# Attention of the first query block and of the sample dealt into the input projection; the sample's tokens in the first block; values by features

## The chip, the cores and the metric

One core of a Trainium2 chip runs the whole program in one launch. Its engines are TensorE (PE; its weight loads are listed as PEld), VectorE (DVE), ScalarE (ACT), GpSimd (POOL) and SyncE (SP), which issues the DMAs. The metric is the device time of one execution in microseconds, the median of several runs.

## The reference

One layer of a hybrid encoder on 2048 prompt tokens and 32 sample tokens (model width 1024), all in f32:

```
h = x + RMSNorm(Mixer(RMSNorm(x)))
y = h + RMSNorm(ConvFFN(RMSNorm(h)))
Mixer:  proj = RMSNorm(x) @ w_in            -> q, k, v (512 each), z (512), xbc (768), dt (8)
  A: stick-breaking attention, 8 heads of 64: w = sigmoid(z_ij) * prod_{j<l<i} sigmoid(-z_il)
     prompt queries see earlier prompt keys, sample queries 2048 cached keys and earlier sample keys
  B: SSD: xbc -> causal conv (4 taps), SiLU -> x, B, C;  dt = softplus(dt + bias);
     h_t = exp(dt a) h + dt x B^T;  y = C h + D x;  y * silu(z), RMSNorm
  out = concat(RMSNorm(A), B) @ w_out
ConvFFN: (gelu(conv3(x @ w_gate)) * (x @ w_up)) @ w_down, hidden width 2816
```

Returned are y, the keys and values, the SSM state and the convolution histories, for prompt and sample.

## The kernel before

The 2080 tokens are handled in four blocks (`SBS`): three of 512 and a last one of 544, whose final 32 are the sample's. Activations lie by features: 128 features on the partitions, tokens along the free dimension. Every f32 operand is split into a high part and a rest (`xhi`, `xlo`, `whi`, `wlo`), and a product unit (`dense`, L118) takes 128 output features as 8 × 3 matmuls: for each of the 8 slices of the input width high × high, high × rest and rest × high. A 544-token block needs them twice, over 272 tokens each. `weight` (L98) loads such a unit's 512 KB into `wraw`, ACT rounds it to the high part (L108), POOL subtracts (L109).

The **input stage** (`phase_in`) does for each block: the split into parts (L272 f.); six units of `wbx` with the convolution and SiLU behind each (L324–346); the values and dt by tokens, the tokens of 128 being the stationary operand and 260 columns of `wv` moving (L365); the steps from dt to the cumulated decay, stored to DRAM (`acD`) and loaded back as a broadcast (`acB`, L426); SSD over four blocks of 128 tokens (L421–514): the decay matrix is `acB` minus `acum` (DVE L436), its exponential (ACT L440), times the masked C·B (L455, L458), then the products with x (L486) and the new state (`hT`, L498, L510), which the next block needs; the next block's squares, norm and normalisation in place (`prep`, L263); four units of `wk` and four of `wq`, each stored to DRAM; four units of `wz` with the gate (L557) and the gated norm. The last block's gate is not done there. It becomes a filler.

**Attention** then takes the blocks of queries one after the other (`heads`, L782). A slot is one head, 512 keys and 128 queries: two score matmuls into `z` (L811), two sigmoids on ACT (L659, L660), a reversed product scan on DVE (L662), a product on POOL or DVE (L667). Two slots later (`LOOK`) follow the transposes into `pt` (L832), a copy and, once per head, the value matmuls into `pa` (L847). Between slots `fill` hands out dense matmuls of the filler: the last gate under block 0, and under block s + 1 the output projection and feed-forward net of block s (`Tail.stream`). `sample` (L670) takes one step at every third slot of block 0. The last block's tail runs alone.

The order on each engine is made by a scheduler from this program order and the pools, except where `pin` ties filler matmuls to attention's. PSUM has eight banks of 512 columns: `o` has two for dense products; `in_psm` (`st`) two and `in_psy` (`y`) two of double size in the input stage; `z`, `pt` two each, `pa` and `u` one each in attention.

## Time and profile before

| | us |
|---|---|
| median of 3 runs (lowest, highest) | 3002.01 (3001.19, 3012.61) |
| profiled execution | 2999.56 |
| its span | 2997.4 |
| PE, DVE, ACT, POOL busy | 2839.3, 1567.7, 1239.6, 1254.8 |
| granted TensorE clock, mean | 0.979 |
| input stage of the four blocks | about 0 to 628 |
| heads of block 0, sample, last gate, first output products | about 628 to 800 |
| move to the tail of block 0 under block 1's heads | about 800 to 905 |
| heads of blocks 1 to 3 over the tails of blocks 0 to 2 | about 905 to 2478 |
| tail of block 3 alone | about 2478 to 2997 |

A row of a group reads: line, engine, operation, written tile <- read tiles, shapes, count | busy us, mean ns of one | idle us of the engine just before them and what ended it. A timeline row has start, duration, engine, line. A row of the chain has start, the time spent on the path, engine, tile, line. Matmuls are pipelined, so a mean of one in a group is longer than the distance at which they follow each other.

### The profile page before, as it was taken

To read this page: it belongs to the slowest core of one execution; us is meant where nothing else is said; L and a number is where in the kernel's file an instruction comes from. 1 tells how busy PE (TensorE), PEld (TensorE's weight loads), DVE (VectorE), ACT (ScalarE), POOL (GpSimd) and SP (SyncE) were. 2 spreads that over 40 slices of the span, in tenths; PEclk is the share of its full clock that TensorE was granted. 3 is DMA by queue.
4 is the path that set the end of the run, shared out by engine and by line. 5 is a ranking of instruction groups with operands and counts; after the bars stand their busy time and mean duration, and the time that the engine had idled before them with its cause. 6 is when DMAs were issued, how large, how long until landed. Compare 5 with 4: busy or idle time off the path is not lost.

```text
span 2997.4 us, 43276 instructions
## 1 busy us (share of the span) xinstructions
PE 2839.3 (95%) x16175; PEld 2320.3 (77%) x16175; DVE 1567.7 (52%) x2386; ACT 1239.6 (41%) x2514; POOL 1254.8 (42%) x1077
## 2 busy tenths in 40 slices
PE   8999899989979999999999999999999999899996
PEld 6777778866757778886677777856777779799996
DVE  7676676546574544337734344485444543523334
ACT  5344444346675544337533333564333433312111
POOL 4555555245666665536522222454122224511113
PEclk9999999989989999999999999999999999899998
DMA  5645453657657777876455545645544455554555
GB/s 172 183 145 177 144 169 106 185 150 248 241 178 242 246 250 266 289 265 203 158 190 176 184 156 208 232 163 174 177 165 167 157 196 191 192 188 167 178 178 171
DMA packets 234659, 571.58 MB, mean 191 GB/s; under 512 B 49514, under 2 KB 101362, under 8 KB 205906
## 3 DMA queue, kind: packets, MB, share of 16 engines
q1 hardware_dynamic: 234450, 568.81, 57.2%
q8 instruction: 129, 2.11, 0.3%
q14 instruction: 80, 0.66, 0.1%
HBM read 435.22 MB, written 133.50 MB: 190 GB/s over the span
## 4 chain that ended last, share of the span: by engine, by line
PE 72%; DVE 14%; DMA 6%; issue 3%; ACT 3%; POOL 2%; SPq 1%; DVEq 0%; POOLq 0%; ACTq 0%
PE o L124 36%; PE u L124 11%; PE t L124 10%; PE pa L847 4%; PE z L811 3%; PE pt L832 3%; DVE prow L662 2%; PE o L365 2%; DVE xc L341 2%; DVE acB L436 1%; DMA xr<-hS 1%; DMA acB<-acD 1%; DVE xc L337 1%; DVE x L263 1%; DMA w<-wS_out 1%
## 5 line engine op out<-in xcount | busy, mean ns | idle before, releaser
L124 PE MATMUL o<-xhi,w 128*128 128x512 f32 (+2 forms) x3968 | 1039.6, 346 | 28.4 <-ACT xhi L287 7.9
L124 PEld LDWEIGHTS o<-xhi,w 128*128 128x128 f32 x3968 | 696.5, 191 | 129.6 <-issue 10.1
L124 PE MATMUL o<-xlo,w 128*128 128x512 f32 (+2 forms) x1984 | 684.9, 345 | 9.4 <-DVE xlo L959 4.1
L109 POOL TENSOR_TENSOR w<-wraw,w 128x1024 fp32r<-128x1024 f32 (+2 forms) x156 | 370.6, 2376 | 256.1 <-ACT w L108 233.3
L124 PEld LDWEIGHTS o<-xlo,w 128*128 128x128 f32 x1984 | 379.6, 191 | 56.8 <-DVE xlo L959 7.6
L667 POOL TENSOR_TENSOR beta<-beta,prow 128x512 f32<-128x512 f32 (+3 forms) x256 | 255.7, 1000 | 377.4 <-DVE prow L662 345.2
L124 PE MATMUL u<-xhi,w 128*128 128x512 f32 x1056 | 345.8, 398 | 0.8 <-ACT r L201 0.5
L124 PE MATMUL o<-ah,w 128*128 128x512 f32 x992 | 335.9, 401 | 3.3 <-ACT f L1057 2.6
L1013 POOL TENSOR_TENSOR y<-y,gb 128x512 f32<-128x512 f32 (+1 forms) x88 | 115.5, 1313 | 511.2 <-ACT gb L1012 509.2
L662 DVE TENSOR_TENSOR_SCAN prow<-gam,prow,z 128x513 f32<-128x513 f32 x192 | 244.8, 1277 | 108.7 <-ACT beta L660 103.2
L124 PEld LDWEIGHTS u<-xhi,w 128*128 128x128 f32 x1056 | 198.5, 188 | 56.1 <-issue 5.6
L659 ACT ACTIVATE gam<-z 128x512 f32<-128x512 f32 (+2 forms) x320 | 173.3, 542 | 128.1 <-PE z L811 83.0
L124 PEld LDWEIGHTS o<-ah,w 128*128 128x128 f32 x992 | 187.1, 189 | 49.8 <-ACT f L1057 3.6
L124 PE MATMUL u<-xlo,w 128*128 128x512 f32 x528 | 209.3, 396 | 0.0
L835 ACT COPY wt<-pt 128x512 f32<-128x512 f32 (+3 forms) x282 | 148.1, 532 | 144.0 <-PE pt L832 141.3
L1005 DVE SCALAR_TENSOR_TENSOR y<-gb,cv,y 128x512 f32<-128x512 f32 (+1 forms) x176 | 162.3, 923 | 78.4 <-ACT y L1003 75.6
L108 ACT CAST w<-wraw 128x1024 fp32r<-128x1024 f32 (+2 forms) x156 | 155.2, 995 | 114.5 <-PE o L124 63.7
L124 PE MATMUL o<-al,w 128*128 128x512 f32 x496 | 196.5, 396 | 0.0
L124 PE MATMUL t<-xhi,w 128*128 128x272 f32 x960 | 189.1, 292 | 2.3 <-DMA w<-wS_up 2.0
L832 PEld LDWEIGHTS pt<-ident,beta 128*128 128x128 f32 x1088 | 132.4, 144 | 67.8 <-issue 27.5
L832 PE MATMUL pt<-ident,beta 128*128 128x128 f32 x1088 | 177.4, 282 | 6.4 <-POOL beta L667 3.9
L124 PE MATMUL t<-ah,w 128*128 128x272 f32 (+1 forms) x768 | 160.1, 302 | 17.4 <-ACT f L1057 7.5
(262 smaller groups left out, 4845.9 us busy)
## 6 DMA issues: line engine op xcount, KB each, us to landing
w<-wS_up SPq DMA_DIRECT2D x132, 1024.0 KB, 4.8
w<-wS_dn SPq DMA_DIRECT2D x72, 768.0 KB, 4.8
wS_up<-w SPq DMA_DIRECT2D x44, 1024.0 KB, 4.8
w<-wS_out SPq DMA_DIRECT2D x39, 1024.0 KB, 6.3
wraw<-wup SPq DMA_DIRECT2D x44, 512.0 KB, 5.9
k<-kS SPq DMA_DIRECT2D x80, 256.0 KB, 4.0
wS_dn<-w SPq DMA_DIRECT2D x24, 768.0 KB, 4.5
w<-wS_dn SPq DMA_DIRECT2D x32, 512.0 KB, 4.4
```

Source lines behind the costliest of these rows:

```text
L108: nc.scalar.copy(hi[:, :n, :], raw[:, :n, :])
L109: nc.gpsimd.tensor_tensor(lo[:, :n, :], raw[:, :n, :], hi[:, :n, :].bitcast(F32), op=ALU.subtract)
L124: mm = nc.tensor.matmul(ps[:, : c1 - c0], l[:, k, :], at(r, k0 + k)[:, c0:c1], start=first and i == 0 and k == 0, stop=last and i == 2 and ...
L659: nc.scalar.activation(g[:, c0:512], z, AF.Sigmoid, scale=-0.125)
L662: nc.vector.tensor_tensor_scan(back(pr), back(g), z[:, 0:1].to_broadcast([P, n + 1]), self.kn.ones[:, 0:1] if prev is None else prev, op0= ...
L667: eng.tensor_tensor(b[:, :n], b[:, :n], pr[:, c0 + 1 : 513], op=ALU.mult)
L811: mm = nc.tensor.matmul(z[:, :n], q[:, P * b : P * b + P], k[:, :n], start=e == 0, stop=e == 1 and kc < s)
L832: mm = nc.tensor.transpose(t[:, P * j : P * j + P], w[:, P * j : P * j + P], kn.ident[:])
L835: copy(wt[:, : n // P, P * b : P * b + P], t[:, :n].rearrange("p (i q) -> p i q", q=P))
L847: nc.tensor.matmul(av[DH * (j % 2) : DH * (j % 2) + DH, c0:], v[:, j, :], wt[:, j, c0:], start=kc == s and j < 2, stop=kc == 0 and j > 1,)
L1005: nc.vector.scalar_tensor_tensor(y[:, :W], gb[:, i : i + W], kn.col(wc + i), y[:, :W], op0=ALU.mult, op1=ALU.add)
L1013: nc.gpsimd.tensor_tensor(y[:, :W], y[:, :W], t, op=ALU.mult)
```

## The change

- The sample's 32 tokens move from the last block to the first (`SBS`, `SS`), so its keys and queries exist after block 0.
- `Attention` is made before the input stage, and `phase_in` is a generator that yields after every unit of products: 0 in block 0, `RATE` = 0.66 in blocks 1 to 3. For each whole sum, `build` takes one step of `early`: sample attention, then the slots of block 0's heads. What is left is done behind the stage. `z` and `pt` have one bank each until then, two afterwards.
- The SSD tiles have one buffer for two, `st` and `y` one bank for two.
- x is loaded twice, slice by slice: once in `ahead` for the squares of the next block, once in `take` for the parts, which are scaled by the gain alone. The norm `r` multiplies each product on its way out of PSUM on DVE (`leave`), which was an ACT copy. The first tap of the convolution goes from DVE to ACT.
- Values are made by features like the keys, four units of `wv`, and transposed on TensorE (through `st`) for attention; dt has 16 columns of its own (`wdt`: high part and rest).
- One unit of `wk` stands behind each SSD block, then come values, gate, queries, for all four blocks alike. Eight units of `w_out` are split and stored during blocks 1 and 2.
- In the tail, the second tile of an up product uses a bank of `o`.

```diff
+RATE = 0.66
...
-SBS = [(0, 512), (512, 512), (1024, 512), (1536, 544)]
+SBS = [(0, 544), (544, 512), (1056, 512), (1568, 512)]
 NSB = len(SBS)
+SS = 0
 
...
-    ep = pool("in_early", 1)
-    sd = pool("in_ssd", 2)
+    xcp = pool("ssd_out", 1, side="right")
+    sd = pool("in_ssd", 1)
     c1p = pool("in_const", 1)
     rp = pool("in_r", 1)
-    tmp = pool("in_tmp", 2)
+    tmp = pool("in_tmp", 6)
     so = pool("in_out", 2)
     wp = kn.wp
-    psm = pool("in_psm", 2, space=PSUM)
-    psy = pool("in_psy", 2, space=PSUM)
+    psm = pool("in_psm", 1, space=PSUM)
+    psy = pool("in_psy", 1, space=PSUM)
     psd = kn.po
...
-        r = kn.rstd_narrow(rp, psm, "st", [sq], nt, D)
-        for k in range(KC):
-            nc.vector.scalar_tensor_tensor(
-                x[:, k, :nt], x[:, k, :nt], kn.col(C_GMIX + k), r[:, :nt], op0=ALU.mult, op1=ALU.mult
-            )
-        return x
-
-    def split(s, x):
...
+            square(sq, load(s, k), k == 0)
+        return root(s, sq)
...
-            nc.scalar.copy(xhi[k][:, :nt], x[:, k, :nt])
-            nc.vector.tensor_tensor(
-                xlo[k][:, :nt], x[:, k, :nt], xhi[k][:, :nt].bitcast(F32), op=ALU.subtract
-            )
-        return xhi, xlo
...
+        def leave(src, name):
+            dst = so.tile([P, 544], F32, name=name)
+            for ps, c0, c1 in product(src):
+                nc.vector.tensor_tensor(dst[:, c0:c1], ps[:, : c1 - c0], r[:, c0:c1], op=ALU.mult)
+            return dst
...
-                nc.scalar.copy(raw[:, c, 3 + c0 : 3 + e], ps[:, : e - c0])
...
+                nc.vector.tensor_tensor(raw[:, 3 + c0 : 3 + e], ps[:, : e - c0], r[:, c0:e], op=ALU.mult)
...
+            nc.scalar.activation(y, raw[:, 0:W], AF.Identity, scale=kn.col(wc), bias=kn.col(C_SB + c))
...
+            for k in range(KC):
+                nc.tensor.matmul(
+                    ps[:16, : c1 - c0], wdt[:, k, :], xhi[k][:, c0:c1], start=k == 0, stop=False, skip_group_check=True
+                )
+                nc.tensor.matmul(
+                    ps[:8, : c1 - c0], wdt[:, k, 0:8], xlo[k][:, c0:c1], start=False, stop=k == KC - 1,
+                    skip_group_check=True,
+                )
+            nc.vector.tensor_tensor(dtr[:16, c0:c1], ps[:16, : c1 - c0], r[:16, c0:c1], op=ALU.mult)
...
-            vp = [psd.tile([P, 512], F32, name="o") for _ in range(2)]
-            for h in range(2):
-                for k in range(KC):
-                    for i, (l, rr) in enumerate(((xhi, wv[0]), (xlo, wv[0]), (xhi, wv[1]))):
-                        nc.tensor.matmul(
-                            vp[h][:q, :260], l[k][:, b * P : b * P + q], rr[:, k, h * 260 : h * 260 + 260],
-                            start=i == 0 and k == 0, stop=i == 2 and k == KC - 1,
-                        )
...
+        fill = keys("wk", kn.kS)
+        for b in range(nb):
+            ssd_block(kn, s, b, sd, psm, psy, triu, dt, te, dec, acum, xcA, xcB, hS if b == 4 else None, hT, state)
+            if b == nb - 1 and not last:
+                nxt = ahead(s + 1)
+            yield next(fill, 0.0)
...
+        for c in range(4):
+            if s in (1, 2):
+                out = 4 * s - 4 + c
+                kn.weight(wp, a["wout"][out], key=("out", out))
+            vf = leave(a["wv"][c], "kf")
+            nc.sync.dma_start(o["vT"][c * P : c * P + P, t0 : t0 + nt], vf[:, :nt])
+            ps = psm.tile([P, 512], F32, name="st")
+            for b in range(4):
+                nc.tensor.transpose(ps[:, b * P : b * P + P], vf[:, b * P : b * P + P], kn.ident[:])
+            vt = so.tile([P, 544], F32, name="khi")
+            nc.scalar.copy(vt[:, :512], ps[:])
...
+        for c in range(4):
+            z = leave(a["wz"][c], "kf")
+            t = tmp.tile([P, 550], F32, name="t")
+            nc.scalar.activation(t[:, :nt], z[:, :nt], AF.Sigmoid)
...
+        yield from keys("wq", kn.qS)
...
-        self.pz = inside("at_pz", 2, space=PSUM)
-        self.pt = inside("at_pt", 2, space=PSUM)
-        self.pa = inside("at_pa", 1, space=PSUM)
...
+    def banks(self, ctx, n):
+        pool = lambda name, bufs: ctx.enter_context(
+            self.kn.tc.tile_pool(name=name, bufs=bufs, reuse_waits="tile", space=PSUM)
+        )
+        self.pa, self.pz, self.pt = pool("at_pa", 1), pool("at_pz", n), pool("at_pt", n)
...
-                prev[g] = carry[g][:]
-                nc.scalar.copy(prev[g], end)
+                w, prev[g] = self.weights_of(z[:, :n], n, prev[g])
+                yield
...
-        ssd = ExitStack()
-        kn.xcp = ssd.enter_context(tc.tile_pool(name="ssd_out", bufs=1, reuse_waits="tile", side="right"))
+        kn.wp, kn.wbufs = enter(tc.tile_pool(name="weights", bufs=1, reuse_waits="tile")), WBUFS
+        att = Attention(kn, enter(ExitStack()))
         with ExitStack() as c2:
-            kn.wp, kn.wbufs = c2.enter_context(tc.tile_pool(name="weights_in", bufs=1)), 2
-            rest = phase_in(kn, c2)
-        kn.wp, kn.wbufs = enter(tc.tile_pool(name="weights", bufs=1, reuse_waits="tile")), WBUFS
+            att.banks(c2, 1)
+            early = chain(att.sample(c2), att.slots(0, 0))
+            debt = 0.0
+            for n in phase_in(kn, c2):
+                debt += n
+                while debt >= 1:
+                    debt -= 1
+                    next(early, None)
+            for _ in early:
+                pass
+            out = att.out
         pu = enter(tc.tile_pool(name="psum_u", bufs=1, space=PSUM))
-        heads = enter(ExitStack())
-        att = Attention(kn, heads)
+        att.banks(att.inner, 2)
         kn.bank = pu, "u"
-        late = ssd.enter_context(tc.tile_pool(name="ssd_tmp", bufs=2, reuse_waits="tile", side="right"))
-        att.filler, normed = rest(lambda nm: late.tile([P, 544], F32, name=nm, bufs=1 if nm == "sq" else 2), late)
-        with ExitStack() as c2:
-            sample = att.sample(c2, pu)
-
-            out = att.heads(0, KC * 4, lambda i: i % 3 == 2 and next(sample, None))
-            for _ in sample:
-                pass
-        for _ in normed:
-            pass
-        ssd.close()
         tail = Tail(kn, att, ctx, pu)
         for s in range(NSB):
             att.filler = tail.stream(s, att.norm_in(s, *out))
```

Three places in the order. The first is TensorE at the program's start: products of `wbx` in block 0, and the sum of squares (`st<-ones,sq`) from which the norm comes. Before:

```order
L124 MATMUL o<-xlo_176,w 128x512
L124 MATMUL o<-xhi_168,w 128x512
L124 MATMUL o<-xhi_161,w 128x512
L124 MATMUL o<-xlo_169,w 128x512
L166 MATMUL st<-ones,sq 128x1 x4
L124 MATMUL o<-xhi_161,w 128x512
```

And in the change, where the norm's broadcast (`st<-ident,rn_v`) follows at once:

```order
L126 MATMUL o<-xlo_215,w 128x272
L126 MATMUL o<-xhi_207,w 128x272
L154 MATMUL st<-ones,sq 128x1 x4
L154 MATMUL st<-ones,sq 32x1
L183 MATMUL st<-ident,rn_v 128x128 x4
L183 MATMUL st<-ident,rn_v 128x32
L126 MATMUL o<-xhi_200,w 128x272
```

48 matmuls of 512 tokens stood ahead of the sum of squares and the third product began ahead of the broadcast; now 48 of half the width stand ahead of both, and the second product behind both.

The second is TensorE late in the SSD of the third block (`y` and `st` are SSD's tiles, `pa`, `pt`, `z` attention's, `o` a dense product). Before:

```order
L124 MATMUL o<-xhi_2881,w 128x512
L498 MATMUL st<-xw,bT 64x256 x2
L469 MATMUL st<-ident,xc 128x128 x3
L486 MATMUL y<-acB,xdt 64x128 x8
L446 MATMUL y<-xc 128x128
L469 MATMUL st<-ident,xc 128x128
L124 MATMUL o<-xlo_2889,w 128x512
L124 MATMUL o<-xhi_2881,w 128x512
```

In the change:

```order
L538 MATMUL y<-acB,xdt 64x128 x8
L521 MATMUL st<-ident,xcA 128x128 x4
L805 MATMUL pa<-wt,v 64x512 x2
L805 MATMUL pa<-wt,v 64x256
L805 MATMUL pa<-wt,v 64x128
L790 MATMUL pt<-ident,beta 128x128
L769 MATMUL z<-k,qa 128x384
L769 MATMUL z<-k,qb 128x384
L773 LDWEIGHTS identb
L773 MATMUL z<-maskq,identb 128x128
L498 MATMUL y<-xcB 128x128
L500 MATMUL y<-xcB,hT_191 128x128 x2
```

Products stood on both sides of an SSD block's matmuls; now attention's do, and in that place no dense product stands among some 50 rows.

The third is ACT in an SSD stretch (L440 and L441, now L492 and L493, are the exponentials of the decay; L619 and L620 attention's sigmoids). Before:

```order
L441 ACTIVATE eA<-eA 128x512
L440 ACTIVATE acB<-acB 128x1024
L441 ACTIVATE eA<-eA 128x512
L440 ACTIVATE acB<-acB 128x1024
L305 COPY kf<-o 128x512
L532 CAST khi<-kf 128x512
L108 CAST w<-wraw 128x1024
```

In the change:

```order
L493 ACT_TABLE_LOAD
L493 ACTIVATE eA<-eA 128x512
L677 COPY wt<-pt 128x512
L395 CAST khi<-kf 128x512
L619 ACT_TABLE_LOAD
L619 ACTIVATE gam_141<-z 128x512
L620 ACTIVATE beta<-z 128x512
L110 CAST w<-wraw 128x1024
L492 ACT_TABLE_LOAD
L492 ACTIVATE acB<-acB 128x1024
```

Exponentials of several SSD blocks stood together; now sigmoids stand between them, each time with a table load. Over the program there are 50 table loads for 24.

580 lines of the change are left out of this document (257 added, 323 removed).

## The prediction

> **What bounds the kernel now.** I read the page's totals first, then the chain that ended last, then the busy time by stretch, because an average over stages says nothing about one stage.
>
> ```profile
> PE 2839.3 (95%) x16175; PEld 2320.3 (77%) x16175; DVE 1567.7 (52%) x2386; ACT 1239.6 (41%) x2514; POOL 1254.8 (42%) x1077
> PE 72%; DVE 14%; DMA 6%; issue 3%; ACT 3%; POOL 2%; SPq 1%; DVEq 0%; POOLq 0%; ACTq 0%
> 0.00:628.00 628.00, 582.94 (x3504) 488.61 (x3505) 415.69 (x709) 269.15 (x427) 302.50 (x177) 0.98 0.51 156
> 628.00:800.00 172.00, 151.27 (x1043) 112.48 (x1042) 103.59 (x147) 117.25 (x281) 107.10 (x119) 0.95 0.69 224
> 800.00:905.00 105.00, 88.54 (x520) 64.08 (x519) 69.33 (x91) 67.67 (x161) 61.45 (x71) 0.92 0.65 212
> 905.00:2478.00 1573.00, 1539.13 (x7446) 1184.76 (x7445) 777.00 (x996) 669.22 (x1394) 647.28 (x576) 0.99 0.60 203
> 2478.00:2997.40 519.40, 477.46 (x3672) 470.38 (x3670) 202.08 (x444) 116.30 (x253) 136.48 (x136) 0.97 0.53 178
> ```
>
> The stretch rows give, after its bounds and length, busy time of PE, weight load, DVE, ACT and POOL, then granted clock, DMA share and GB/s. TensorE bounds the program, so a change pays only where it takes matmuls away or closes a hole between them. The long stretch 905 to 2478 has few holes. The 172 us after the input stage (heads of block 0, sample attention, last gate) and the 105 us behind them do, and their clock is lower. Busy time of a matmul includes its wait in the pipeline, so I price PE work by rows in which matmuls run back to back:
>
> ```profile
> 1184.52 22.34 PE o L124 x96
> 2638.39 6.03 PE o L124 x48
> 214.97 8.85 PE o L365 x72
> 652.14 0.60 PE L832 MATMUL pt<-ident,beta 128*128 128x128 f32 x4
> 654.82 1.50 PE L847 MATMUL pa<-wt,v 128*64 128x512 f32 x8
> ```
>
> That is 22.34/96 = .233 us for a matmul over 512 tokens, .126 over 272, .123 for the value product's 260 columns, at most .15 for a transpose and 1.5 for a head's eight widest value matmuls.
>
> **1. TensorE work.** Values by tokens go: 4 blocks of 192 matmuls and 48 for the sample, 816 × .123 = −100.4. Values by features come: 96 per 512-token block, 192 of 272 in the first, 3 × 96 × .233 + 192 × .126 = +91.3. The dt columns now need matmuls of their own, 16 per tile: 48 × .233 + 32 × .126 = +15.2. The 16 to 17 transposes a block plus those of dt, about 85, cost at most .15, +12.8. Sum **+19** (+15 if transposes pack at .1, +21 as upper end). Everything else on TensorE is moved, not changed; 544 tokens move from the last block to the first at equal price.
>
> **2. Heads of block 0 and sample attention.** What does TensorE do in those 172 us?
>
> ```profile
> L124 PE MATMUL o<-xhi,w 128*128 128x272 f32 x133 | 33.8, 316 | 1.2 <-POOL w L109 1.2
> L832 PE MATMUL pt<-ident,beta 128*128 128x128 f32 x157 | 27.2, 292 | 0.9 <-DVE rn_v L176 0.5 <-DVE wt L835 0.4
> L124 PE MATMUL o<-xhi,w 128*128 128x256 f32 x113 | 23.2, 294 | 1.7 <-DMA xhi<-yS 0.8 <-ACT xhi L760 0.8
> L847 PE MATMUL pa<-wt,v 128*64 128x512 f32 x60 | 16.6, 612 | 1.4 <-ACT wt L835 1.4
> L710 PE MATMUL z<-sk,qp 128*64 128x32 f32 x8 | 1.4, 262 | 6.6 <-DMA sk<-kF 6.6
> L811 PE MATMUL z<-k,qa 128*128 128x512 f32 x23 | 10.9, 475 | 4.0 <-DVE prow L662 4.0
> ```
>
> The counts (the low-part products are half of the high-part ones) at back-to-back prices: dense products 45, transposes 24, values 15, scores and masks 23, sample 19, norms 5, together 131. So 172 − 131 = 41 us were not covered: the chain score, sigmoid, scan, product, transpose has too little dense work beside it. In the change those 44 steps (10 sample, 34 slots) go out at .66 per yield over 69 yields, so none remains when the input stage ends, and each stands between products of about 5.6 us. Their matmuls still cost what they cost. **−41**; the bounds are −30, if a fifth to a quarter of the holes is the move to the output projection, which stays, and −41.
>
> **3. The start.** Before, a product's exit copies raw sums, and TensorE runs two 512-token products of 24 ahead of the norm.
>
> ```profile
> 24.57 0.39 PE L124 MATMUL o<-xlo,w 128*128 128x512 f32 x1
> 24.81 0.95 PE L166 MATMUL st<-ones,sq 128*128 128x1 f32 x8
> L260 POOL TENSOR_TENSOR sq<-sq,t 128x544 f32<-128x544 f32 x7 | 9.6, 1367 | 12.3 <-ACT t L259 11.8
> ```
>
> Now each exit multiplies by the norm, and the first product of 544 tokens fills both PSUM banks, so the second must wait for the norm; its squares are added on POOL, seven at 1.367 us. About one product of 6 us is not done ahead, and the norm's root (three to five us behind the last add) is bare: **+8**, between 0 and +12.
>
> **4. The SSD stretches.** Here the change speaks against itself: its tiles go from two buffers to one, its two PSUM pools from two banks to one, because attention now needs banks as well. Block 1 before:
>
> ```profile
> 228.86 0.19 DVE L391 SCALAR_TENSOR_TENSOR ab<-u 128x32 f32<-128x32 f32 x1
> 246.88 6.47 DMA acB<-acD
> 249.16 3.77 DVE L436 TENSOR_SCALAR acB<-acB,acum 128x128 f32<-128x128 f32 x8 [7.40 <-DMA acB<-acD]
> 262.83 0.69 DVE L493 TENSOR_TENSOR xc<-y,xc 128x512 f32<-128x512 f32 x1
> 290.61 0.68 DVE L493 TENSOR_TENSOR xc<-y,xc 128x512 f32<-128x512 f32 x1
> L440 ACT ACTIVATE acB<-acB 128x1024 f32<-128x1024 f32 x16 | 17.0, 1060 | 57.8 <-DVE acB L436 57.8
> ```
>
> From dt to the first decay matrix 20.3 us pass (small steps, a store and a broadcast load), then the first and fourth block's last addition (262.83 and 290.61) put the blocks (290.61 − 262.83)/3 = 9.3 us apart. With one acB the next broadcast may start only when the eight state products of the block before have read it: 5 to 6.5 us of load, 3.8 of DVE, 1.06 of ACT, about 2 of masks and products, 12.3 in all with no queueing; 16 with a queue. So a stretch is 20 + 4 + 4 × (12.3 to 16) + 4 for the next norm's root: 77 to 92 us. The cover is eight products (45 us), SSD's own matmuls (about 20) and dealt attention (6 to 20, none in block 0, where seven units of 6.03 and five SSD blocks make 66 against 84 to 90). That leaves 45 to 55 us of holes over four blocks, since the third value product cannot leave PSUM before the single bank passes to the transposes, behind the whole chain. Before, 0 to 628 holds 386 us of dense products (54 × 5.6 + 14 × 6.03), 100 of values and some 85 of SSD and norms (four blocks at 20, and the roots); less the lead of 8 and 5 of cold clock, 44 are stalls, 9 of them at block ends (part 5), so 35 here. 50 − 35: I take **+15**. Below: the chain at 9.3 as now, overlapped but for 5 us, −30. Above: 16 us in every block and no cover from attention, +60. The 12.3 is nearest to the rows, so the value lies low in that range.
>
> Of the holes the worst had a second price:
>
> ```profile
> 604.99 0.28 PE L480 MATMUL st<-ident,xc 128*32 128x128 f32 x1 [3.33 <-DVE hT L510]
> 611.42 0.66 PE L124 MATMUL o<-xhi,w 128*128 128x272 f32 x2
> 618.82 0.42 PE L124 MATMUL o<-xhi,w 128*128 128x272 f32 x2
> ```
>
> After 3.33 us of idle TensorE, pairs of matmuls took .66, then .42 again by 618.8: some 5 us lost. The Trainium skill, page "TensorE: Matmul & The Clock Gate", section "What's actually happening", has the clock halve after about one idle window of 3.4 us and return after another 3.4 of work; the trace agrees on the gap and shows a longer return, about ten us. By the page a long hole costs 1.7 us more, by the row five. Attention's matmuls stand in most of the new holes, so the sum counts no cold stretch beyond the one there is.
>
> **5. Ends of blocks.** These waits go:
>
> ```profile
> 148.40 9.61 DVE x L263 x8
> 298.77 7.53 DVE x L263 x8
> 460.85 8.32 DVE x L263 x8
> L124 PE MATMUL o<-xhi,w 128*128 128x512 f32 x864 | 282.9, 406 | 17.1 <-ACT xhi L287 7.9 <-DVE t L576 5.6 <-POOL w L109 2.4
> L124 PE MATMUL o<-xlo,w 128*128 128x512 f32 x432 | 175.4, 406 | 4.7 <-DVE xlo L273 3.6 <-DVE xlo L288 1.1
> L365 PE MATMUL o<-wvhi,xhi 128*128 128x260 f32 x256 | 73.3, 286 | 8.7 <-ACT v L374 4.3 <-ACT v L372 1.8 <-ACT raw L330 1.7
> ```
>
> The gate's exits (5.6 us idle), the low parts (3.6) and the value exits (8.7, counted already in part 4's stalls by half) are the visible part; the query products now stand between gate and block end, and x is no longer normalised in its place (25 us of DVE over three blocks). **−12**, between 0 (all of it returns at the parts of the next block, which still need eight loads, ACT and DVE) and −25, the sum of the DVE rows.
>
> **6. Behind the input stage.** The count that paces the filler of block 1's heads is 1152, but the stream has 1098 steps, so three of 64 slots run bare: **+4** (0 to +8). The last block's tail shrinks by 32 tokens and the first one's grows by as many: 0. Splitting eight output-weight units early is ACT and POOL work under dense products: 0; without that cover 8 × 3.4 = 27.
>
> **Sum**: +19 − 41 + 8 + 15 − 12 + 4 = −7. Against the profiled execution, 2999.56 (span 2997.4), 2992.6; the median shown is 2.4 above the profiled one, so **2995 us**, the same as before within the 0.5% (15 us) that a measurement tells from no change.
>
> **Rivals.**
>
> *A, the SSD chain disappears under products.* Attention is dealt exactly there and eight products follow; if of 50 us of holes only 5 stay, part 4 is −30 instead of +15: 2950. It needs a period under about 10 us. For it: DVE is 52% busy, and the chain row of block 1 lay beside products almost without idle TensorE. Against it: two buffers then, one now.
>
> *B, the one-buffer chain decides.* Scans and exits come to DVE.
>
> ```profile
> 305.00:462.00 157.00, 101.51 (x167) 0.98 0.51 155
> L303 DVE TENSOR_TENSOR kf<-o,r 128x512 f32<-128x512 f32 x8 | 5.5, 683 | 2.2 <-PE o L124 2.2
> ```
>
> The first row is DVE alone in one block: 101.5 − 9.2 of normalising + 14 exits × .683 + about 20 of scans and copies is about 122 us. If each of the four SSD steps waits in that queue and the period is 16 us, 17 blocks cost 3.7 more each, 63, and a quarter is hidden: some +45, 3040. It decides from a period of about 13.5 us, where the holes eat the gain of part 2.
>
> *C, the activation tables.* Sigmoid now alternates with exp inside each stretch, and the order has 50 table loads for 24.
>
> ```profile
> 229.49 1.28 ACT L392 ACT_TABLE_LOAD   x1
> 230.79 0.23 ACT L392 ACTIVATE e<-ab 128x32 f32<-128x32 f32 x1
> ```
>
> 26 × 1.28 = 33 us of ACT. Those ahead of an exp of acB lengthen the chain of part 4 directly; three quarters of them there give +25: 3020. It decides when the load is issued after the DVE row has ended, not in the idle time ahead of it. The Trainium skill, page "ScalarE: Activation LUTs", section "What ACT_TABLE_LOAD costs", adds about 1.38 us of drain to the 1.28; the row does not agree, since the activation begins 1.30 after the load. By the page the case would give some 50 instead of 25.
>
> **How the numbers follow.** The forecast, 2975 to 3015, gets 0.40; A 0.32, because an overlapped chain is what block 1 shows; B 0.16; C 0.12. Of the forecast's share 0.12 lies below 2987. Faster is 0.32 + 0.12 = 0.44, within 0.5% 0.28, slower 0.16 + 0.12 = 0.28. The range takes all the forecast, most of A and of B: 2940 to 3045; the forecast's own is 2975 to 3015.
>
> **What would show it.** Part 1: dense matmuls of values and dt with 85 more transposes in the groups. Part 2: no row of scores between the input stage and the output projection of block 0, and PE busy at or above 95% in the second half of each block. Part 3: first norm's broadcast ahead of the second product, which starts near 27 us. Part 4: distance of the y additions in blocks 1 to 3, 12 to 13 us by the forecast, under 10 by A, 16 by B; holes on TensorE ended by the decay, the state or the value's transposes. C: table loads directly behind the DVE row of the decay. The forecast is wrong if the holes between the first product of block 0 and the last query of block 3 sum to under 25 us or over 85.

## The result, and the profile after

| | before | after |
|---|---|---|
| median us | 3001.6 (4 runs, 2998.93 to 3012.61) | 3098.81 (4 runs, 3091.8 to 3100.76) |
| ratio after / before | | 1.0312, 95% interval 1.0282 to 1.0343 |
| span of the profiled execution | 2997.4 | 3090.0 |
| mean granted TensorE clock | 0.979 | 0.970 |

The change made the kernel 3.1% slower, some 97 us, where 2995 us was forecast. The end of the range was 3045.

The profile's totals and the shares of the chain, of the kernel after:

```profile
PE 2881.3 (93%) x16142; PEld 2340.0 (76%) x16142; DVE 1616.4 (52%) x2456; ACT 1278.7 (41%) x2511; POOL 1297.2 (42%) x1099
PE 67%; DVE 12%; DMA 7%; issue 5%; ACT 4%; POOL 4%; SPq 1%; DVEq 0%; POOLq 0%; ACTq 0%
```

TensorE is still the busiest, but its share of the chain fell from 72 to 67%. The busy time by stretch tells where. The first view is the kernel after, the second the kernel before cut at corresponding places (those of the kernel after lie up to 6 us behind the first step of dt): the start, the chain from dt of block 0, 1, 2, 3 to its last SSD block, and in the last two rows the first tail under heads and the lone tail. The columns are those of the prediction's stretch rows.

```profile
0.00:88.00 88.00, 64.30 (x429) 59.88 (x429) 51.12 (x89) 38.00 (x64) 39.01 (x37) 0.86 0.36 119
88.00:165.00 77.00, 61.07 (x449) 53.82 (x449) 49.14 (x128) 21.64 (x33) 33.32 (x21) 0.85 0.49 151
290.00:390.00 100.00, 82.60 (x477) 57.69 (x476) 68.62 (x110) 51.06 (x69) 52.85 (x32) 0.92 0.72 241
509.00:600.00 91.00, 74.85 (x394) 53.44 (x393) 67.05 (x126) 63.39 (x95) 53.30 (x40) 0.87 0.71 222
708.00:792.00 84.00, 71.49 (x372) 51.49 (x370) 53.99 (x116) 40.19 (x61) 35.77 (x24) 0.88 0.51 155
839.60:1488.00 648.40, 618.46 (x4596) 563.42 (x4595) 320.66 (x509) 317.82 (x670) 358.24 (x291) 0.99 0.70 236
2589.30:3090.00 500.70, 457.68 (x2248) 379.34 (x2248) 191.22 (x318) 113.68 (x235) 138.31 (x146) 0.97 0.60 199
```

```profile
0.00:79.00 79.00, 65.74 (x367) 56.17 (x368) 53.55 (x72) 39.91 (x61) 33.77 (x24) 1.00 0.51 170
79.00:140.00 61.00, 58.98 (x336) 44.75 (x335) 46.78 (x107) 22.48 (x33) 30.75 (x18) 1.00 0.64 196
230.00:292.00 62.00, 59.12 (x336) 44.65 (x335) 45.35 (x100) 26.08 (x40) 33.09 (x21) 1.00 0.63 190
387.00:449.00 62.00, 59.62 (x334) 45.34 (x333) 47.66 (x101) 25.77 (x40) 31.78 (x21) 0.97 0.64 191
549.00:620.00 71.00, 63.44 (x489) 57.01 (x488) 47.36 (x121) 24.43 (x46) 27.75 (x19) 0.90 0.59 172
726.60:1367.00 640.40, 610.30 (x3174) 479.69 (x3173) 320.88 (x407) 324.52 (x666) 383.06 (x309) 0.98 0.72 246
2459.60:2997.40 537.80, 494.16 (x3768) 484.64 (x3764) 208.50 (x459) 120.41 (x262) 144.34 (x145) 0.96 0.55 186
```

An SSD stretch of blocks 1 to 3 took 62 to 71 us and takes 84 to 100. Its clock was 0.90 to 1.00 and is 0.87 to 0.92. Most of the loss is there. It comes with idle time, with a slower clock, and with less dense work to cover it: 179 dense matmuls stand in the stretch of block 1 where 187 stood, and 149 in that of block 2 where 183 stood.

To separate work from loss I priced every matmul record of both traces at the distance at which its form follows when TensorE waits for nothing (0.23 us over 512 tokens, 0.125 over 272, 0.12 over 260, 0.09 for a transpose, and so on). What is left of a stretch is uncovered: idle time, slow clock and the drains between. In us:

| part of the program | before: length, work, uncovered | after: length, work, uncovered |
|---|---|---|
| start to dt of block 0 | 79, 60, 19 | 88, 52, 36 |
| SSD of block 0 | 61, 55.5, 5.5 | 77, 50, 27 |
| rest of block 0 | 22, 20, 2 | 55, 47, 8 |
| blocks 1 to 3 without SSD | 271, 245.5, 25.5 | 344.6, 308.2, 36.4 |
| SSD of blocks 1 to 3 | 195, 166, 29 | 275, 184, 91 |
| heads of block 0, sample, last gate | 98.6, 69.6, 29 | 0 |
| sum up to the first heads of block 1 | 726.6, 617, 109 | 839.6, 642, 198 |
| tails under heads | 1733 | 1749.7 |
| last tail alone | 537.8 | 500.7 |

So 113 us are lost up to the first heads of block 1: 25 of work and 89 uncovered. The remaining 20 come back behind them (17 more under the heads, 37 less alone), which gives the 93 us between the spans.

The last step of an SSD block, the addition of y, in block 1 of the kernel after; the times are the start of the first and the last of four:

```profile
L545 DVE TENSOR_TENSOR xcA<-y,xcA x4: 665/680/692, 326.7 to 387.0; 128x512 f32<-128x512 f32 x4
```

(387.0 − 326.7)/3 = 20.1 us a block, where it was 9.3. In blocks 2 and 3 it is 16.9 and 16.4.

### The profile page after: what moved, and what is told of

Its sections match the earlier page's. It is cut to its first block, busy times and chain, and to the rows that moved or that the text cites. A ratio compares the mean times of both kernels' runs of the same rounds, so it can differ in the third digit from the quotient of the medians.

```text
span 3090.0 us, 43496 instructions
## 1 busy us (share of the span) xinstructions
PE 2881.3 (93%) x16142; PEld 2340.0 (76%) x16142; DVE 1616.4 (52%) x2456; ACT 1278.7 (41%) x2511; POOL 1297.2 (42%) x1099
## 4 chain that ended last, share of the span: by engine, by line
PE 67%; DVE 12%; DMA 7%; issue 5%; ACT 4%; POOL 4%; SPq 1%; DVEq 0%; POOLq 0%; ACTq 0%
PE o L126 37%; PE t L126 9%; PE u L126 9%; PE pa L805 4%; PE z L769 3%; PE pt L790 3%; DVE prow L622 2%; DMA acB<-acD 1%; DVE xcA L312 1%; POOL w L111 1%; DVE acB L488 1%; DMA xr<-xT 1%; DVE f L1040 1%; DMA t<-xT 1%; ACT w L110 1%
## 5 line engine op out<-in xcount | busy, mean ns | idle before, releaser
L126 PE MATMUL o<-xhi,w 128*128 128x512 f32 (+2 forms) x4640 | 1202.2, 343 | 33.4 <-DVE kf L293 11.1
L126 PEld LDWEIGHTS o<-xhi,w 128*128 128x128 f32 x4640 | 810.9, 192 | 146.6 <-DVE kf L293 12.6
L126 PE MATMUL o<-xlo,w 128*128 128x272 f32 (+2 forms) x2320 | 794.9, 343 | 13.5 <-DVE xlo L263 7.2
L627 POOL TENSOR_TENSOR beta<-beta,prow 128x512 f32<-128x512 f32 (+4 forms) x264 | 265.3, 1006 | 449.8 <-DVE prow L622 409.8
L126 PE MATMUL o<-ah,w 128*128 128x272 f32 (+1 forms) x1344 | 362.0, 344 | 10.6 <-DVE f L1019 6.7
L126 PE MATMUL u<-xhi,w 128*128 128x512 f32 (+1 forms) x1056 | 300.9, 362 | 0.6 <-ACT r L189 0.5
L619 ACT ACTIVATE gam<-z 128x512 f32<-128x512 f32 (+3 forms) x330 | 178.6, 542 | 131.0 <-PE z L769 77.5
L126 PE MATMUL o<-al,w 128*128 128x272 f32 (+1 forms) x672 | 227.3, 338 | 0.0
L126 PE MATMUL u<-xlo,w 128*128 128x512 f32 (+1 forms) x528 | 190.3, 360 | 0.0
L620 ACT ACTIVATE beta<-z 128x512 f32<-128x512 f32 (+3 forms) x330 | 178.6, 541 | 0.0
```

The source lines that it names most:

```text
L126: mm = nc.tensor.matmul(ps[:, : c1 - c0], l[:, k, :], at(r, k0 + k)[:, c0:c1], start=first and i == 0 and k == 0, stop=last and i == 2 and ...
L619: nc.scalar.activation(g[:, c0:512], z, AF.Sigmoid, scale=-0.125)
L620: nc.scalar.activation(b[:, :n], z, AF.Sigmoid, scale=0.125)
L627: eng.tensor_tensor(b[:, :n], b[:, :n], pr[:, c0 + 1 : 513], op=ALU.mult)
```

## The experiments

The names of the theories are those of the expectations: 1, the dealt attention steps lengthen SSD; 2, the single buffers and banks do (2a the reload of the decay, 2b the banks); 3, the activation tables. Every ratio is against the kernel before, measured beside it.

### Nothing dealt

```diff
-RATE = 0.66
+RATE = 0.0
```

> The changed kernel with a rate of 0: no step of attention is dealt into the input stage; sample and heads of block 0 all follow behind it, with one bank each and nothing beside them. Theory 1 (the dealt steps lengthen SSD): the additions of y in blocks 1 to 3 stand about 12 us apart as they do in block 0 of the changed kernel (11.9), not 16 to 20, and the four blocks together end some 100 us earlier than they do now (840 us), by the attention work that left (about 76 us) and by 12 shorter SSD steps. Theory 2 (single buffers): the distance stays at 16 or more. The whole becomes slower in both, by 50 to 120 us, since the 44 steps lie bare behind the stage.

3102.09 us, ratio 1.0344 (1.0327 to 1.0362), the same as the change. The y additions of block 1 stand (380.7 − 331.5)/3 = 16.4 us apart. But the run doesn't tell what it was made for: the first score of block 0's heads comes at 393 us, as in the change (387). Five of the sample's scans stand in the SSD of block 1 in both runs. The scheduler places the steps beside the products as soon as their banks and data are there; where the program text hands them out hardly matters.

### No step between SSD blocks

```diff
-RATE = 0.66
+RATE = 0.85
...
-            yield next(fill, 0.0)
+            next(fill, None)
+            yield 0.0
```

> The changed kernel, but no step is dealt between the SSD blocks of blocks 1 to 3 (yields there give 0), and 0.85 instead of 0.66 at every other unit, so that all steps still go out before the stage ends. Theory 1 (dealt steps lengthen SSD): distance of the y additions 12 us in all blocks, 40 to 60 us faster than the change, about 3040 to 3060. Theory 2 (single buffers set the distance): it stays at 16 or more, the time stays within 20 us of the change or rises, since the stretch has lost its attention work.

3094.03 us, 1.0314 (1.0295 to 1.0332); y additions 15.5 us apart in block 1 (333.7 to 380.3), first score at 375 us. The same answer as above, for the same reason: the order was hardly changed.

### Single buffers and banks in the kernel before

```diff
-    sd = pool("in_ssd", 2)
+    sd = pool("in_ssd", 1)
...
-    psm = pool("in_psm", 2, space=PSUM)
-    psy = pool("in_psy", 2, space=PSUM)
+    psm = pool("in_psm", 1, space=PSUM)
+    psy = pool("in_psy", 1, space=PSUM)
```

> The kernel before with the SSD tiles in one buffer, and one bank each for st and y, nothing else: what the loss of buffers costs by itself. Theory 2 (single buffers): the distance of the y additions goes from 9.3 to 16 us, and as in the prediction's upper case the time rises by 40 to 60 us, to 3040 to 3060. Theory 1: distance about 12 us, rise of at most 20 us.

3068.43 us, 1.0228 (1.0213 to 1.0244): 67 us, above what theory 2 expected. Nothing else of the change is in this kernel. Its y additions in block 1, by the timeline:

```profile
L493 DVE TENSOR_TENSOR xc<-y,xc x4: 692/693/694, 286.0 to 346.0; 128x512 f32<-128x512 f32 x4
```

20.0 us apart on the mean, 18 in the first two steps. The timeline of SP, DVE and PE in that stretch shows the step that the prediction's sum of 12.3 us lacked:

```profile
299.35 1.09 PE L486 MATMUL y<-acB,xdt 128*64 128x128 f32 x16
302.35 1.63 DVE L490 SCALAR_TENSOR_TENSOR xc<-xc,cv,eA 128x128 f32<-128x128 f32 x2
304.01 1.28 SPq L432 DMA_DIRECT2D eA<-acD  x2
307.31 0.38 SPq L426 DMA_DIRECT2D acB<-acD  x1
312.20 2.70 DVE L436 TENSOR_SCALAR acB<-acB,acum 128x128 f32<-128x128 f32 x8 [6.25 <-DMA acB<-acD]
```

The products that read acB end at 300.4, and it could be loaded again. But in SP's order eA's load stands ahead of acB's, and it waits for the last reader of eA on DVE (ended 303.98). With two stores and a weight load between, acB's load is issued at 307.3, 7 us after its release, and the first DVE step follows at 312.2. Over blocks 1 and 2 of this run the delay is 3 to 8 us; in the change it is 3 to 6 us in block 1 and 0 to 4.5 in blocks 2 and 3.

### Banks alone, then each bank

```diff
-    psm = pool("in_psm", 2, space=PSUM)
-    psy = pool("in_psy", 2, space=PSUM)
+    psm = pool("in_psm", 1, space=PSUM)
+    psy = pool("in_psy", 1, space=PSUM)
```

> The kernel before with one bank each for st and y, but two buffers for all SSD tiles in SBUF. With everything single the y additions stood 18.2 us apart and the time rose by 67 us. Theory 2a (the reload of the decay: eA's load stands ahead of acB's in SP's queue and waits for the last reader of eA, so the next acB lands about 12 us after its release): two buffers remove it, distance 9 to 11 us, at most 15 us slower than before. Theory 2b (the banks): distance 15 us or more, 40 to 67 us slower.

3044.91 us, 1.0146 (1.0128 to 1.0164): 45 of the 67 us are the banks', with SSD's tiles in SBUF in two buffers. Then one of the two lines at a time, for y and for st:

> The kernel before with one bank pair for y, two for st. One bank for both cost 45 us and put the y additions 20 us apart. If y is the one (its next C B product has to wait for the addition that reads the last one, and then all steps follow in a row): distance 17 us or more, 30 to 45 us slower. If st is: distance 9 to 12, under 10 us slower.

> The kernel before with one bank for st, two pairs for y. If y is the one that costs, distance 9 to 12 us and under 10 us slower; if st is (the transposes of x, B, the state and the next norm pass through it one by one), 17 us or more and 30 to 45 us slower. If both are needed for it, each alone costs under half of 45.

y alone: 3005.75 us, 1.0016 (1.0002 to 1.0031). st alone: 3032.27 us, 1.0112 (1.0094 to 1.0129). The timeline's count of the y additions of block 1 with both single:

```profile
L493 DVE TENSOR_TENSOR xc<-y,xc x4: 677/693/694, 277.5 to 329.9; 128x512 f32<-128x512 f32 x4
```

The same with y single:

```profile
L493 DVE TENSOR_TENSOR xc<-y,xc x4: 683/692/694, 273.2 to 316.8; 128x512 f32<-128x512 f32 x4
```

And with st single:

```profile
L493 DVE TENSOR_TENSOR xc<-y,xc x4: 674/693/695, 275.5 to 326.7; 128x512 f32<-128x512 f32 x4
```

17.5, 14.5 and 17.1 us. One pair for y lengthens the chain by half and costs only 5 us; one bank for st costs 32. Through st pass, in every SSD block, the transposes of x, that of B and the new state, and then the next block's norm; DVE and ACT read it in turn.

By the pricing of the table above, st's 32 us do not lie in the SSD stretches (some 42 us uncovered there, 40 before) but between them (60, where it was 28). The longer chain draws in more products, about 72 us of work in the stretch of block 1 where 55 stood. So the next block's norm, which passes the same bank behind the last state, has fewer products beside it. TensorE at the end of block 1 of that run:

```profile
332.63 0.94 PE L166 MATMUL st<-ones,sq 128*128 128x1 f32 x8
335.81 1.16 PE L195 MATMUL st<-ident,rn_v 128*128 128x128 f32 x8 [2.23 <-POOL rn_v L184]
339.32 1.22 PE L124 MATMUL o<-xhi,w 128*128 128x512 f32 x2 [2.36 <-ACT xhi L272]
```

With y single the stretches between have 22 us uncovered, no more than before.

### Two decays in the change

```diff
-    acB = sd.tile([P, 8, P], F32, name="acB")
+    acB = sd.tile([P, 8, P], F32, name="acB", bufs=2)
...
-    eA = sd.tile([P, 4, P], F32, name="eA")
+    eA = sd.tile([P, 4, P], F32, name="eA", bufs=2)
...
-    tmp = pool("in_tmp", 6)
+    tmp = pool("in_tmp", 3)
```

> The changed kernel with two buffers for acB and eA alone (three instead of six for t, which pays for them). Theory 2a: distance of the y additions in blocks 1 to 3 falls from 16 to 20 to about 12 us, the time by 40 to 60 us (3040 to 3060). Theory 2b: distance at 15 or more, less than 20 us gained.

3086.8 us, 1.0284 (1.0269 to 1.0299), 12 us better than the change by the medians, 8 by the ratios, whose intervals overlap. Its y additions in block 1:

```profile
L545 DVE TENSOR_TENSOR xcA<-y,xcA x4: 668/683/694, 326.4 to 370.6; 128x512 f32<-128x512 f32 x4
```

14.7 us in block 1 instead of 20.1. The reload is a part of the chain, not all of it, and shortening it gained little.

### st and pt share two banks, alone and with two decays

`st` and attention's `pt` are taken from one pool of two banks in turn; the second run adds the edit above.

```diff
-    psm = pool("in_psm", 1, space=PSUM)
+    psm = kn.psm
...
-        self.pa, self.pz, self.pt = pool("at_pa", 1), pool("at_pz", n), pool("at_pt", n)
+        self.pa, self.pz, self.pt = pool("at_pa", 1), pool("at_pz", n), pool("at_pt", 2)
```

> The changed kernel in which st and attention's pt share two banks in turn, where each had one. In the kernel before, one bank for st alone cost 32 us and y alone 5. If st's single bank is also the larger part here, distance of the y additions in blocks 1 to 3 under 15 us and 20 to 35 us faster than the change. If the dealt transposes take the second bank whenever it is free, or the other single tiles hold the chain, under 10 us.

> The shared banks together with two buffers for acB and eA (three for t instead of six). Two decays alone gained 12 us. If bank and decay each hold the chain in turn, as in the kernel before (45 us by banks, 67 with the tiles), the two together gain more than the sum, 40 to 60 us: 3040 to 3060. If the stretch is bound by TensorE's order and its clock, the sum at most.

3093.39 us, 1.0305 (1.0285 to 1.0324), and 3078.12 us, 1.025 (1.0224 to 1.0276). The shared banks alone are within the error of the change; with the decays they bring 20 us against it, which within the errors is the sum of the two (5 and 12), not the 40 to 60 that were expected if both hold the chain in turn. The y additions of blocks 1 to 3 stand 15.3 and 13.1 us apart on the mean. A second bank for `st` alone is not there: `o` 2, `y` 2, `st`, `z`, `pt` and `pa` take the eight banks that the kernel shares out.

### Exponentials without a table of their own

```diff
-    nc.scalar.activation(acB[:q, :, :q], acB[:q, :, :q], AF.Exp)
-    nc.scalar.activation(eA[:, :, :q], eA[:, :, :q], AF.Exp)
+    nc.scalar.activation(acB[:q, :, :q], acB[:q, :, :q], AF.Sigmoid)
+    nc.scalar.activation(eA[:, :, :q], eA[:, :, :q], AF.Sigmoid)
```

> The changed kernel with both large exponentials of each SSD block replaced by the sigmoid that attention uses (the decay factors are then other numbers), so that no table changes inside the SSD stretch. Theory 3 (the table loads are on the chain, rival C): some 24 loads of 1.28 us go, each on the SSD chain, distance of the y additions 2 to 3 us shorter, 20 to 40 us faster. Theories 1 and 2: less than 10 us.

3090.33 us, 1.0303 (1.0285 to 1.0322), 8 us under the change and within both intervals; the y additions stand 16.9 us apart on the mean of blocks 1 to 3, where it was 17.8. The table loads of the kernel after, by line:

```profile
L619 ACT ACT_TABLE_LOAD x19 | 24.4, 1283 | 0.3
L493 ACT ACT_TABLE_LOAD x8 | 10.3, 1283 | 21.7 <-DMA eA<-acD 21.6
L492 ACT ACT_TABLE_LOAD x6 | 7.7, 1283 | 17.0 <-DVE acB L488 13.8 <-issue 3.2
```

and of this run:

```profile
L619 ACT ACT_TABLE_LOAD x5 | 6.4, 1283 | 0.1
L493 ACT ACT_TABLE_LOAD x2 | 2.6, 1283 | 8.5 <-DMA eA<-acD 8.5
```

26 loads less, 33 us of ACT, worth at most some 8 us. Rival C is out as a main cause. In the trace after, a load ahead of acB's exponential (six of 17) does stand behind DVE's step, not in the idle time before it, so its 1.28 us lie on the chain, as rival C said; six of them are 8 us.

### Raw exits at the start

In block 0 the units of `wbx` leave PSUM by ACT copies and are multiplied by the norm in SBUF.

```diff
+                if s == 0:
+                    nc.scalar.copy(raw[:, 3 + c0 : 3 + e], ps[:, : e - c0])
...
+                    continue
                 nc.vector.tensor_tensor(raw[:, 3 + c0 : 3 + e], ps[:, : e - c0], r[:, c0:e], op=ALU.mult)
```

> The changed kernel, but in block 0 the six units of wbx leave PSUM raw by ACT copies and the norm multiplies them in SBUF, as before the change. If the wait for the norm holds TensorE at the start, products run on from 24 us, and the second one no longer starts near 36; gain 15 to 20 us, the prediction's part 3 being then 8 us for what is 20. If only a shift (block 0's SSD or its holes take it back): under 8 us.

3095.71 us, 1.0321 (1.0299 to 1.0343): nothing measurable. The second product does begin ahead of the norm, but the third then waits 4.8 us (45.4 us): its bank is freed by ACT copies that stand, in ACT's order, behind the norm's own copies, the first convolution tap, a table load and a sigmoid. dt is ready at 89 us, as in the change. The hole was moved from one product to the next.

### Banks in turns

Attention's banks and its sample buffers are opened when the last SSD block of block 3 is done; until then SSD has two buffers and two banks, and all 44 steps are meant for the last twelve units.

```diff
-    psm = pool("in_psm", 1, space=PSUM)
...
+    psm = pool("in_psm", 2, space=PSUM)
+    inner = ExitStack()
+    sd = inner.enter_context(tc.tile_pool(name="in_ssd", bufs=2, reuse_waits="tile"))
+    psy = inner.enter_context(tc.tile_pool(name="in_psy", bufs=2, reuse_waits="tile", space=PSUM))
...
+            inner.close()
+            yield None
+            rate = 44 / 12
```

> The changed kernel with the banks in turns: SSD has two buffers and two banks again (t four instead of six), attention's banks are opened when the last SSD block of block 3 is done, and all 44 steps are dealt over its last twelve units (values, gate, queries, 67 us of products). If single buffers and banks are what the change pays for, distance of the y additions 9 to 11 us, input stage with attention ends near 740 instead of 840 us, time 2995 to 3020. If what remains (products of values and dt, exits on DVE, start) weighs more than thought, 3030 to 3060.

3158.75 us, 1.0521 (1.0502 to 1.0539), the opposite of what was expected, and worse than the change. The chain is as before the change, by the timeline's count of the y additions in block 1:

```profile
L549 DVE TENSOR_TENSOR xcA<-y,xcA x4: 678/680/693, 317.5 to 346.2; 128x512 f32<-128x512 f32 x4
```

9.6 us a block. The time went behind it:

```profile
702.00:799.00 97.00, 80.82 (x415) 54.63 (x413) 32.85 (x39) 31.83 (x56) 33.92 (x25) 0.89 0.72 229
799.00:903.00 104.00, 67.93 (x263) 37.12 (x262) 42.31 (x72) 42.83 (x111) 24.47 (x39) 0.66 0.26 76
```

The longest of its waits in the second of these stretches is TensorE's for the scan (us in total, times, longest):

```profile
PE z L773 <- DVE prow L626: 21.2, 14, 1.9
```

The heads did not get among the twelve products. The sample's steps stand ahead of them in the program and use the same single bank of z; the sample's last score comes at 795 us and the first of the heads at 799, when the products are done. So the heads lie bare from 799 to 903, with 32 us of work in 104 and a granted clock of 0.66. The scan for which TensorE waits reads z, so the single bank has its share in this. 32 slots without cover and with one bank cost 72 us, where in the kernel before sample, heads and gate together left 29 uncovered. The run therefore tells what two buffers do to the SSD, but not what the change would cost with them.

The same with single buffers and banks again:

> As the run with the banks in turns (attention opened after the last SSD block; y additions 9.6 us apart), but with single tiles and banks for SSD again, so that only the buffers differ. Theory 2 (buffers): distance 15 to 18 us with no attention in the stretch, input stage of blocks 1 to 3 longer by 30 to 60 us, and the time over 3180. Theory 1 (dealt steps): distance 10 to 12 us and within 20 us of that run (3159); the 16 to 20 of the change would then be attention's.

3193.34 us, 1.0645 (1.0609 to 1.0682), 35 us over the run above. Its y additions in block 1:

```profile
L549 DVE TENSOR_TENSOR xcA<-y,xcA x4: 692/694/694, 329.2 to 372.4; 128x512 f32<-128x512 f32 x4
```

14.4 us in block 1, 13.7 and 14.1 in blocks 2 and 3, with no attention in the stretch. This pair shows what the first two runs could not: single buffers take the distance from 9.5 to 14.1 us, and in the change, where attention stands between, it is 17.8 on the mean of its three blocks (20.1, 16.9, 16.4). By the distance both theories hold, buffers for somewhat more than half.

The distance is not the loss, however. The same pricing, with cuts at the first step of dt and at the last y addition of each run, gives what is uncovered, in us (good to a few us):

| kernel | SSD of block 0 | SSD of blocks 1 to 3 |
|---|---|---|
| before | 6 | 34 |
| banks in turns | 17 | 59 |
| the same with single buffers and banks | 29 | 96 |
| the change | 30 | 92 |

Single buffers and banks make 49 us of it, from 76 to 125. The dealt attention makes none: against the run without it the three stretches are 28 us longer and hold 32 us more work. And 36 us stay with two buffers, two banks, no attention in the stretch and y additions 9.5 us apart, where the kernel before has 40 and this run 76. What makes these 36 was not tested. In block 1 of that run the long waits of TensorE in the stretch are for the small steps from dt (4.9 us), the state (3.3) and the decay (3.1).

### The sample in block 0, alone

The kernel before with the change's block sizes and its edits in the tail; the sample's attention result enters block 0's heads when the last of its steps is done.

```diff
-SBS = [(0, 512), (512, 512), (1024, 512), (1536, 544)]
+SBS = [(0, 544), (544, 512), (1056, 512), (1568, 512)]
...
+            for c, t in enumerate(out[0]):
+                nc.vector.tensor_copy(t[:, 512:544], att.att_s[:, c, :])
+                att.square(out[1][:, 512:544], t[:, 512:544], c == 0)
```

> The kernel before with one part of the change alone: the sample's 32 tokens in block 0 instead of block 3, with the tail's edits that go with it (second tile of an up product in a bank of o; the last down products by halves). In the changed kernel everything from the first heads of block 1 to the end takes 16 us less than before, though part 6 of the prediction expected 4 more. If that is due to the sample's place and the tail, this kernel is faster than before by 5 to 20 us (2981 to 2996). If it came from what the change brings into the tail (output weights split early, or the scheduler's other order), 0 to 5 us, or slower because block 0's SSD has five blocks.

3025.11 us, 1.0083 (1.0064 to 1.0101): 25 us slower, against the expectation. Its stretches from the first heads of block 1 on:

```profile
733.00:1415.00 682.00, 642.17 (x4655) 579.47 (x4654) 334.58 (x538) 330.32 (x694) 381.56 (x306) 0.96 0.68 227
2506.00:3025.00 519.00, 478.53 (x2324) 394.30 (x2321) 197.01 (x325) 119.93 (x247) 143.99 (x150) 0.96 0.57 195
```

The tail of block 0 grew from 640 to 682 us, the lone one shrank from 538 to 519. Moving 32 tokens is not the even trade that the prediction made of it.

### The early split of output weights

Out of the change, and alone into the kernel before (there ahead of each query unit of blocks 1 and 2, with a third weight buffer):

```diff
-            if s in (1, 2):
-                out = 4 * s - 4 + c
-                kn.weight(wp, a["wout"][out], key=("out", out))
```

> The changed kernel without the early split of eight output-weight units in blocks 1 and 2 (they are loaded and split under the heads of block 1 again, as before). The prediction put the early split at 0. If that is right, within 8 us of the change. If it is what makes the tail of block 0 short (from the first heads of block 1 to the end of the tail work under them the change takes 648 us for 640 although 32 tokens, 31 us, were added, while the kernel before with the sample moved takes 682), 20 to 35 us slower than the change.

> The kernel before with that early split alone: in blocks 1 and 2 one unit of output weights is split and stored ahead of each query unit (three weight buffers instead of two in the input stage). If the early split is worth what the tail of the change suggests, 10 to 35 us faster than before, 2965 to 2990, all of it between 727 and 1367 us. If the transition there is bound by something else (the norm's chain, attention's own waits), within 5 us.

3102.07 us, 1.0335 (1.0315 to 1.0355), 3 us over the change, not to be told from it; and 3020.35 us, 1.0065 (1.0052 to 1.0079), 18 us slower than before. In the latter the stretch from 741 to 1382 us has the same 641 us as before, so nothing was gained, and the input stage ends 14 us later. The early split is worth about nothing in the change and costs in the kernel before.

No kernel of these beats the one before.

## Why the prediction was wrong

The terms of its sum against the table of uncovered time, in us:

| part | predicted | measured |
|---|---|---|
| 1 TensorE work | +19 | +25 |
| 2 heads of block 0 and sample | −41 | −29 |
| 3 start | +8 | +17 |
| 4 SSD stretches | +15 | +83 (21.5 in block 0, 62 in blocks 1 to 3) |
| 5 ends of blocks | −12 | +17 |
| 6 behind the input stage | +4 | −20 |
| sum | −7 | +93 |

**Part 4 is the step that failed**, "the 12.3 is nearest to the rows, so the value lies low in that range". Its mechanism, one acB that makes the blocks wait for each other, is there, but its size was wrong. The part took the length of a stretch less its cover: 77 to 92 us, of which eight products, SSD's own matmuls and attention were to cover 71 to 85. The three stretches came out at 100, 91 and 84 us, on the mean the upper end, and the work in them is 61 us on the mean (184 in 275). So the cover was mis-sized even more than the length. Dense matmuls were 179, 149 and 165 where eight products have 192, and SSD's own matmuls price at some 12 us where 20 stood. Its baseline, 35 us of stalls before, agrees with the 34.5 of the table, but partly by luck: for 0 to 628 us as a whole the prediction had 57 us not covered, and the table has 81.

The runs show three things behind the size. First, the chain has links that the sum of durations lacks. acB's load is issued behind eA's in SP's queue, up to 8 us after its release in the kernel before with single buffers and up to 6 in the change; and st's bank is passed from one short step to the next. The distance of the y additions was 14.1 us with single buffers alone. Second, attention did not fill the holes. It lengthens the stretches by about as much as it brings work (28 us for 32), since its steps also stand in order ahead of SSD's on the other engines. In the stretch of block 1 after, the longest of DVE's waits is this (us in total, times, longest):

```profile
DVE prow L622 <- ACT beta L620: 11.4, 4, 3.7
```

Third, buffers are about half of it, 49 of 85 us by the table at the end of "Banks in turns"; the cause of the other 36 is open. One candidate stands in the change and was not tested by a run: the exits of the products, which went from ACT to DVE. In the SSD of block 0 they are what TensorE waits for most (first row; then TensorE and DVE in order of time):

```profile
PE o L126 <- DVE kf L293: 10.3, 4, 5.2
102.51 5.83 DVE L488 TENSOR_SCALAR acB<-acB,acum 128x128 f32<-128x128 f32 x8 [3.40 <-DMA acB<-acD]
108.26 0.43 DVE L293 TENSOR_TENSOR kf<-o,r 128x272 f32<-128x272 f32 x1
108.75 0.60 PE L126 MATMUL o<-xhi,w 128*128 128x272 f32 x1 [5.23 <-DVE kf L293]
```

The exit stands behind the decay's step in DVE's order, and that step waited for acB's load. So the products that were to cover the chain wait for it.

Of the 91 us uncovered in blocks 1 to 3, 46 are idle, and the other 45 are slow clock and drains; "the sum counts no cold stretch beyond the one there is" did not come true either. By the prediction's own last sign, holes over 85 us between the first product and the last query, it is wrong too: they sum to 100.

**Rival B** was the right kind of case: period 16 us, slower, decided by the one-buffer chain. It got 0.16 and 3040 us. The period that it assumed is what two of three blocks have (16.9, 16.4), but it priced only what exceeds 12.3 us and hid a quarter of that under products. Its ground, waits in DVE's queue, shows in the rows above, but no run tests it alone. **Rival A** fell: it needed a period under about 10 us. **Rival C** is worth at most 8 us.

**Part 2** was mis-sized by a boundary. The stretch 628 to 800 us ended 73 us into the heads of block 1, and 12 of its 41 uncovered us are the move to the output projection. That stays: from the first to the 33rd slot of block 1 it takes 115 us before and 113 after. The prediction had named this bound (−30) and chosen the other end. What was dealt did disappear as forecast, 29 us.

**Part 3** took the wait for the norm for 6 us of work; the timeline after shows two holes ahead of it:

```profile
20.08 0.59 PE L126 MATMUL o<-xlo,w 128*128 128x272 f32 x1 [4.37 <-DVE xlo L263]
30.41 2.06 PE L154 MATMUL st<-ones,sq 128*128 128x1 f32 x10 [6.25 <-POOL sq L242]
```

And the busy time of the ten us behind the first, with most of the second:

```profile
20.00:30.00 10.00, 3.00 (x10) 2.36 (x10) 2.83 (x2) 2.36 (x3) 8.63 (x5) 0.50 0.32 118
```

The squares are added on POOL, which also splits the next weights in between, and the clock in these ten us is 0.50. **Part 5** had the right waits going and missed that others come: between the SSD stretches of blocks 1 to 3 TensorE now waits 6 us for the exits of `wbx` on DVE (L305), nearly 4 for those of dt (L340) and 7 for attention's steps. **Part 1** was 6 us short, which is about what the norms add: 68 small sums of squares and 68 broadcasts stand ahead of block 1's heads, where 34 of each stood (and six wide sums). **Part 6** counted the shift of 32 tokens as 0. The lone tail lost 37 us and the tails under heads gained 17. Moved alone, the same tokens cost 25 us; what makes the tail of block 0 shorter in the change (648 us) than in that run (682) is open; TensorE's work in the two is nearly the same. The early split is not it: without it the stretch has 662 us and the times do not differ.

The expectation that a step stands where the program hands it out fell with the first two runs: rates of 0, 0.66 and 0.85 give the same time within the errors.

## What to carry to other kernels

Before a buffer or a bank is given away, walk one period of the chain that used it through every queue, the DMA queue too, and look for what stands ahead of the reload: the sum of durations is a floor, and here it was 12.3 us where 14 to 20 came out. Count the cover with the same care, by the matmuls that will stand in that stretch: 61 us stood where 71 to 85 were counted. Price the buffers alone first (here three lines, 67 us); against a gain put at 41 us that run would have spoken against the change. Look where the loss comes out: a longer chain also uses up products that covered something behind it. And idle time is too low a measure of what a chain costs: only 46 of the 91 uncovered us are idle.

## What the runs showed of the hardware

The granted clock fell without any single long gap. In the timeline of block 1 after, the two gaps on TensorE ahead of the fall are of 0.72 and 2.29 us:

```profile
373.61 0.55 PE L675 MATMUL pt<-ident,beta 128*128 128x128 f32 x3 [0.72 <-POOL beta L627]
376.68 1.09 PE L680 MATMUL pa<-sv,wt 128*64 128x128 f32 x16 [2.29 <-DMA sv<-cvv]
```

The busy time in stretches of 3.4 us:

```profile
370.90:374.30 3.40, 2.68 (x14) 1.79 (x12) 3.20 (x6) 1.22 (x2) 1.42 (x2) 1.00 1.01 322
374.30:377.70 3.40, 1.11 (x18) 1.02 (x18) 3.40 (x3) 0.00 (x0) 3.11 (x2) 1.00 1.00 378
377.70:381.10 3.40, 2.27 (x6) 0.32 (x3) 1.69 (x9) 1.63 (x2) 0.00 (x0) 0.51 0.77 267
```

TensorE was busy for 1.11 us, a third, of the stretch behind which the clock went from 1.00 to 0.50. The Trainium skill, page "TensorE: Matmul & The Clock Gate", section "What's actually happening", speaks of an idle window of about 3.4 us; no gap here is that long, so by this trace a stretch that is idle in part is enough. That the shape of small matmuls also plays a part can't be excluded from these rows.
